# Out projection: upper half of the columns, first eight heads, as seven block products per pair of K tiles, summed in PSUM

## The chip, the core and the metric

One core of one Trainium2 chip runs the kernel. The metric is the device time of one execution in microseconds (us), as the median of several. TensorE (PE in the profile) multiplies, with its weight loads listed apart (PEld); VectorE (DVE) and ScalarE (ACT) do elementwise work; GpSimd (POOL) and SyncE (SP) here mostly issue transfers, which sixteen DMA engines carry out. PSUM, the memory that TensorE writes, has eight banks of 128x512 float32.

## What is computed

The reference is one decoder layer on 256 rows of 2048 columns: a mixing part and a feed-forward part, each with a norm before and behind it. The change is in the projection that closes the mixing part, the line with `w_out`.

```python
h = rmsnorm(x, pre_mix_gain[layer])
proj = jnp.einsum('bsd,de->bse', h, w_in[layer])
q_sb, k_sb, v_sb, q_dl, k_dl, v_dl = jnp.split(proj, splits, axis=-1)
o_sb = head_rmsnorm(stick_breaking_attention(...), sb_out_gain[layer])   # 8 heads of 128
o_dl = head_rmsnorm(dilated_attention(...), dil_out_gain[layer])         # 8 heads of 128
mixed = jnp.concatenate([o_sb, o_dl], axis=-1)                           # 256 x 2048
mix_out = jnp.einsum('bse,ed->bsd', mixed, w_out[layer])                 # 2048 x 2048
x = x + rmsnorm(mix_out, post_mix_gain[layer])
h = rmsnorm(x, pre_ffn_gain[layer])
f = conv_geglu_ffn(h, w_up[layer], conv_w[layer], conv_b[layer], w_down[layer])
x = x + rmsnorm(f, post_ffn_gain[layer])
```

## The kernel before

**Arithmetic.** Every large float32 product is taken apart. An operand is split into a high part (type fp32r) and the rest (low part), and one product becomes three matmuls: high by high, low by high, high by low. For a weight tile `raw` of 128x1024, ACT makes the high part (`wh`, function `high`, L139) and DVE subtracts it from the raw tile (`wl`, function `low`, L146).

**Staging.** Weights are streamed. The list `chunks` names them in order of use: V columns ("v"), query and key columns of each head ("qk"), out projection ("out", column block c of 512, K group kq of four K tiles), up projection ("up", 86 of them). A chunk is 128x2048, two raw tiles of 512 KB. The main loop takes one chunk at a time; `ahead` loads up to two chunks ahead, on SP's queue (L128), and splits one ahead. The raw tiles turn in a ring of five buffers, `wh` and `wl` in rings of four. A load is issued when its ring buffer has been split; a split waits until TensorE is done with the tile that held its `wh` and `wl` buffers.

**Out projection.** `mm_moving` multiplies one chunk with the mixed heads: `mix` holds their high and low parts with the K dimension on the partitions, 16 K tiles (one for each head) of 256 rows. For each K tile, each half t of the rows and each column block there are three matmuls of 128x512 (L207, L208, L211), 24 in a chunk, added up in one PSUM bank for each (c, t). The chunks run over columns 0 and 1, then 2 and 3. The last two chunks (c=3, kq=2 and 3) are held and done together, rows t=0 first, so that the norm of t=0 runs beside the matmuls of t=1. `rows.squares` (L573, ACT) and `rows.take` (L577, DVE) empty a bank; `update` (L1040) adds the residual `x1`, which was loaded at the start and stayed in SBUF; `turn` transposes it for the up projection. The attention of the last heads still runs in small pieces (`step`) beside the first out chunks; TensorE's order there was fixed when the program was built.

**Down projection and its sums.** The last stage (class `Down`) already uses seven block products in place of eight for pairs of K tiles. It needs sums of weight blocks, which are not in the input. They are made in DRAM, beside the earlier stages: for each pair a tile T13 (SP copies two blocks of 256 KB, `copy_blocks` L727; POOL adds a third block to each with two accumulating DMAs, `add_block` L731) and for some pairs a tile T24 (one copy, then two additions, one behind the other). I call one copy with its two additions a set. `presum`, called once for each chunk from the eighth on, does one step: T13 takes two steps, T24 three. Here there are 34 T13 and 23 T24, 137 steps in all.

Of the kernel before, what the change touches and what calls it, by code (L numbers as in the profile page):

```python
# [24 lines left out]
RAW_BUFS = 5  # L25
# [11 lines left out]
LATE_PAIRS = 2  # L37
HELD = 4
SINGLE_BEHIND = (0, 2, 4, 5, 7, 9, 11, 12, 14)

# [60 lines left out]
def layer_kernel(ctx: ExitStack, tc: tile.TileContext, a, out: bass.AP):  # L101
    nc = tc.nc
# [17 lines left out]
    HALF = 1024  # L120
    LOW_AT = 80

    def load(src, w, piece=HALF):
        raws = []
        for lo in range(0, w, piece):
            n = min(piece, w - lo)
            raw = wpool.tile([P, n], F32, tag="raw", name="raw", bufs=RAW_BUFS, padded_shape=[P, HALF])
            nc.sync.dma_start(raw, src[:, lo:lo + n])  # L128
            raws.append(raw)
        return raws  # L130

    def split(raws, kind):

        return [low(raw, high(raw, kind), kind) for raw in raws]
# [61 lines left out]

    def mm_moving(ps, parts, hi, lo, k0, first, last, ts=(0, 1)):

        k1 = k0
        for i, (wh, wl) in enumerate(parts):  # L200
            n = wh.shape[1] // 512
            for t in ts:
                tc_ = slice(t * P, (t + 1) * P)
                for j in range(n):
                    k = k1 + j
                    ws = wh[:, j * 512:(j + 1) * 512]
                    T.matmul(ps[t], hi[:, k, tc_], ws, start=(first and i == 0 and j == 0), stop=False)  # L207
                    T.matmul(ps[t], lo[:, k, tc_], ws, start=False, stop=False)  # L208
                for j in range(n):
                    k = k1 + j  # L210
                    T.matmul(ps[t], hi[:, k, tc_], wl[:, j * 512:(j + 1) * 512], start=False,  # L211
                             stop=(last and i == len(parts) - 1 and j == n - 1))
            k1 += n
# [17 lines left out]
    for gs in ((0, 1), (2,), (3,)):  # L231
# [6 lines left out]
    for c0, c1 in ((0, 1), (2, 3)):  # L238
        for c, kqs in ((c0, (0, 1, 2)), (c1, (0, 1, 2)), (c0, (3,)), (c1, (3,))) if c0 == 0 else ((2, (0, 1, 2, 3)), (3, (0, 1, 2, 3))):
            for kq in kqs:  # L240
                chunks.append(("out", c, kq, a["w_o"][c, kq], 2048))
    for j in range(FT):
# [5 lines left out]
    def ahead(i, splits=SPLITS):  # L248
        if i + LOADS >= len(chunks):
            down.load(2 * (i + 1 + LOADS - len(chunks)))  # L250
        if i + 1 == len(chunks):
            down.prepare(2)
        while len(raws) < min(len(chunks), i + 1 + LOADS):
            j = len(raws)
            if j in between:
                nc.sync.dma_start(*between[j])
            raws[j] = load(chunks[j][3], chunks[j][4])
        while len(parts_of) < min(len(chunks), i + 1 + splits):
            j = len(parts_of)
            parts_of[j] = split(raws[j], chunks[j][0])  # L260
        return parts_of[i]
# [13 lines left out]
    gpre = small.tile([P, KT], F32, name="gpre", bufs=1, padded_shape=[P, KT + 32])  # L275
    x1 = apool.tile([P, 2, D], F32, name="x1", bufs=1)
    x1_kept = nc.dram_tensor("x1_kept", (S, D), F32, kind="Internal").ap()
# [138 lines left out]

    vts = {}

    banks = []
# [23 lines left out]
    def stick_head(h, qk):  # L443
# [51 lines left out]
        if h == 0:  # L495
            V.tensor_scalar(gain[:, 0:NH], par[:, P_HEAD:P_HEAD + NH], -0.5, None, op0=ALU.mult)
        V.scalar_tensor_tensor(q, po, gain[:, h:h + 1], q, op0=ALU.mult, op1=ALU.mult)
        A.copy(mix[0][:, h, :], q)
        V.tensor_tensor(mix[1][:, h, :], q, mix[0][:, h, :].bitcast(F32), op=ALU.subtract)

# [175 lines left out]
    class Down:  # L676
# [15 lines left out]
        def __init__(self):  # L692
            self.units, self.tiles, self.presums, self.summed = [], [], [], []
            kept = [nc.dram_tensor(f"{n}_kept", (2, NPAIR, 2, P, HALF // 2), F32, kind="Internal").ap() for n in ("t13", "t24")]
            self.sums13, self.sums24, self.ticks = [], [], 0
            for cp in range(2):
# [35 lines left out]

        def presum(self):


            tick = self.ticks
            self.ticks += 1
            n, odd = divmod(tick, 2)
            if n < len(self.sums13):
                t13, blocks, b12 = self.sums13[n]  # L740
                if odd:
                    self.add_block(t13[0], b12)
                    self.add_block(t13[1], b12)
                else:
                    self.copy_blocks(t13, blocks)
                return
            tick -= 2 * len(self.sums13)
            for n, (t24, blocks, t13) in enumerate(self.sums24):
                at = tick - 3 * n
                if at == 0:  # L750
                    self.copy_blocks(t24, blocks)
                elif at == 1:
                    self.add_block(t24[0], t13[0])
                elif at == 2:
                    self.add_block(t24[1], t24[0])

# [199 lines left out]
    for i, (kind, p, s, _, w) in enumerate(chunks):  # L956
# [39 lines left out]
        elif kind == "qk":  # L996
# [7 lines left out]
            if s == 1:  # L1004
                active.append(stick_head(p, qk) if p < 8 else dilated_head(p, qk))
                next(active[-1])
        elif kind == "out":
            if s == 0:
# [4 lines left out]
            if p == 3 and s == 2:  # L1013
                held = parts
                continue
            if p < 3 or s < 2:
                mm_moving(mm["out", p], parts, mix[0], mix[1], 4 * s, s == 0, s == 3)
                if s == 3:
                    for t in range(2):
                        rows.squares(mm["out", p][t], t, p)  # L1020
                        rows.take(mm["out", p][t], t, p)
            else:
# [33 lines left out]
                def lows(b):  # L1056
                    for j in range(2):
# [3 lines left out]
                                                   op0=ALU.mult, op1=ALU.subtract))  # L1061

                for t in range(2):
                    mm_moving(mm["out", p], held + parts, mix[0], mix[1], 8, False, True, (t,))
                    if t == 1:
# [131 lines left out]
def _laid_out(inp):  # L1197
# [14 lines left out]
    for cp in range(2):  # L1212
        for kind, j in _down_plan(cp):
# [8 lines left out]
    w_first = np.concatenate([xT[n[0]] if len(n) == 1 else w_v[n[0], 0, :, n[1] * 512:(n[1] + 1) * 512]  # L1222
                              for names in OPENING for n in names], 1)
    arrays = {
        "x": x,
# [3 lines left out]
        "w_v": w_v,  # L1229
        "w_o": np.asarray(inp["w_out"])[0].reshape(4, 4, P, 4, 512).transpose(3, 0, 2, 1, 4).reshape(4, 4, P, 2048),  # L1230
        "w_up": np.asarray(inp["w_up"])[0].reshape(KT, P, 2, FT, P).transpose(3, 2, 1, 0, 4).reshape(FT, 2, P, 2048),
        "w_dn": w_dn,
# [20 lines left out]
```

## Time and profile before

| what | us |
|---|---|
| median of 3 runs | 1083.21 |
| the three runs | 1082.92, 1083.21, 1100.46 |
| the profiled execution, its whole time | 1082.44 |
| its span, first to last instruction | 1080.7 |
| out projection in that span, about | 293 to 386 |
| up projection, about | 389 to 861 |
| down projection and end, about | 861 to 1081 |

The granted TensorE clock was 0.998 of full speed over the span. A row of the profile's tables gives busy time, the mean duration of one instruction and the idle time before it; matmuls overlap, so the duration of one is more than the distance from one to the next. The three runs spread by 0.3 us without the one at 1100.46.

### The profile page before, as it was taken

What the parts mean: (1) busy time and instruction counts of PE and PEld (TensorE: products, weight loads), DVE (VectorE), ACT (ScalarE), POOL (GpSimd) and SP (SyncE); (2) the same over time, 40 slices, a digit from 0 to 9 for tenths busy, and PEclk for the clock granted to TensorE, in tenths of its full rate; (3) what the DMA queues carried; (4) which work ended last, traced back from release to release, by engine and by line L of the source; (5) the groups of instructions that cost most, each with busy time, mean ns of one, the idle gap of its engine ahead of it and who ended that gap; (6) DMA issues with size and microseconds to landing.
All of it is one profiled execution on the core that took longest, in us unless ns stands there. A gap on an engine that the chain in (4) does not pass through costs nothing.

```text
span 1080.7 us, 18925 instructions
## 1 busy us (share of the span) xinstructions
PE 1069.3 (99%) x7169; PEld 977.6 (90%) x7169; DVE 835.5 (77%) x1267; ACT 676.1 (63%) x991; POOL 96.7 (9%) x127
## 2 busy tenths in 40 slices
PE   9999999999999999999999999999999999999996
PEld 7888888988888889999999999999999988888885
DVE  7577766866865478887877878787787699998997
ACT  6657867756754385555555555555555587666775
POOL 0011111111111101111001001001000000000002
PEclk9999999999999999999999999999999999999999
DMA  9999889899889959998888888888888799779993
GB/s 352 358 289 282 242 239 282 245 271 253 249 259 282 268 207 301 296 285 265 255 262 263 257 248 266 262 255 260 263 243 272 210 340 380 270 265 355 395 361 120
DMA packets 96188, 297.88 MB, mean 276 GB/s; under 512 B 10400, under 2 KB 11168, under 8 KB 91680
## 3 DMA queue, kind: packets, MB, share of 16 engines
q1 hardware_dynamic: 90192, 266.24, 70.4%
q0 software_dynamic: 5472, 29.89, 16.7%
q8 instruction: 56, 0.92, 0.3%
q10 hardware_dynamic: 432, 0.53, 0.1%
q14 instruction: 36, 0.29, 0.1%
HBM read 292.43 MB, written 63.96 MB: 330 GB/s over the span
## 4 chain that ended last, share of the span: by engine, by line
PE 98%; DVE 1%; ACT 0%; issue 0%; DVEq 0%; ACTq 0%
PE mmu L171 42%; PE mmqk L161 11%; PE p L819 6%; PE p L818 6%; PE p L817 6%; PE mmqk L159 5%; PE mmv L207 3%; PE mmv L211 3%; PE mmv L208 3%; PE mmo L211 3%; PE mmo L208 3%; PE mmo L207 3%; PE mmu L182 1%; PE score L441 1%; PE idle L300 0%; PE head L441 0%
## 5 line engine op out<-in xcount | busy, mean ns | idle before, releaser
L146 DVE TENSOR_TENSOR wl<-raw,wh 128x1024 fp32r<-128x1024 f32 (+1 forms) x379 | 452.1, 1200 | 173.2 <-ACT wh L139 142.3
L139 ACT CAST wh<-raw 128x1024 fp32r<-128x1024 f32 (+1 forms) x379 | 389.4, 1033 | 176.4 <-PE mmu L171 60.8
L171 PE MATMUL mmu<-hT,wh 128*128 128x256 f32 x2688 | 311.9, 276 | 0.0
L171 PEld LDWEIGHTS mmu<-hT,wh 128*128 128x128 f32 x2688 | 308.1, 188 | 0.0
L171 PE MATMUL mmu<-hT,wl 128*128 128x256 f32 x1344 | 159.6, 276 | 0.0
L171 PEld LDWEIGHTS mmu<-hT,wl 128*128 128x128 f32 x1344 | 155.7, 188 | 0.0
L161 PE MATMUL mmqk<-hT,wh 128*128 128x512 f32 x512 | 121.8, 390 | 0.0
L161 PEld LDWEIGHTS mmqk<-hT,wh 128*128 128x128 f32 x512 | 94.9, 188 | 19.0
L637 ACT ACTIVATE cv<-pair,par 128x256 f32<-128x256 f32 x86 | 51.6, 600 | 81.2 <-DVE pair L635 80.9
L731 POOL DMA_DIRECT2D t_kept<-in_w x68 | 53.7, 918 | 409.5 <-DMA t_kept<-in_w_dn 409.5
L817 PE MATMUL p<-wh,yp 128*128 128x512 f32 x210 | 81.7, 389 | 0.0
L818 PE MATMUL p<-wh,yp 128*128 128x512 f32 x210 | 81.7, 389 | 0.0
L819 PE MATMUL p<-wl,yp 128*128 128x512 f32 x210 | 81.6, 390 | 0.0
L159 PE MATMUL mmqk<-hT,wl 128*128 128x256 f32 x512 | 67.0, 278 | 0.0
L731 POOL DMA_DIRECT2D t_kept<-t_kept x46 | 35.6, 775 | 338.5 <-DMA t_kept<-in_w_dn 206.1
L159 PEld LDWEIGHTS mmqk<-hT,wl 128*128 128x128 f32 x512 | 63.2, 188 | 1.3
L638 DVE SCALAR_TENSOR_TENSOR cv<-pair,par,cv 128x255 f32<-128x255 f32 x86 | 41.2, 479 | 15.2 <-ACT cv L637 15.2
L207 PE MATMUL mmo<-wh,mix 128*128 128x512 f32 x128 | 50.1, 391 | 0.0
L208 PE MATMUL mmo<-wh,mix 128*128 128x512 f32 x128 | 49.8, 389 | 0.0
L208 PE MATMUL mmv<-wh,hT 128*128 128x512 f32 x128 | 49.7, 390 | 0.0
L207 PE MATMUL mmv<-wh,hT 128*128 128x512 f32 x128 | 49.6, 390 | 0.1
L819 PEld LDWEIGHTS p<-wl,yp 128*128 128x128 f32 x210 | 39.4, 188 | 8.6 <-DVE wl L146 0.4
(242 smaller groups left out, 1290.7 us busy)
## 6 DMA issues: line engine op xcount, KB each, us to landing
raw<-in_w_up SPq DMA_DIRECT2D x172, 512.0 KB, 5.6
raw<-in_w_qk SPq DMA_DIRECT2D x64, 512.0 KB, 6.0
t_kept<-in_w_dn SPq DMA_DIRECT2D x57, 512.0 KB, 6.8
t_kept<-in_w POOLq DMA_DIRECT2D x68, 256.0 KB, 6.6
raw<-in_w_o SPq DMA_DIRECT2D x32, 512.0 KB, 5.6
raw<-in_w_dn SPq DMA_DIRECT2D x31, 512.0 KB, 6.8
raw<-t_kept SPq DMA_DIRECT2D x29, 512.0 KB, 6.6
raw<-in_w_v SPq DMA_DIRECT2D x28, 512.0 KB, 5.7
```

The lines of the kernel that those rows point to most:

```text
L139: pin(A.copy(wh, raw))
L146: pin(V.tensor_tensor(wl, raw, wh.bitcast(F32), op=ALU.subtract))
L159: T.matmul(ps[:, 0, :], w, h[:, k, 0, :], **edge)
L161: T.matmul(ps, w, h[:, k, :, :], **edge)
L171: pin(T.matmul(ps, w, h[:, k, part, :], start=(i == 0), stop=(i == 3 * KT - 1)))
L207: T.matmul(ps[t], hi[:, k, tc_], ws, start=(first and i == 0 and j == 0), stop=False)
L208: T.matmul(ps[t], lo[:, k, tc_], ws, start=False, stop=False)
L211: T.matmul(ps[t], hi[:, k, tc_], wl[:, j * 512:(j + 1) * 512], start=False, stop=(last and i == len(parts) - 1 and j == n - 1))
L731: tc.keep_in_program_order(G.dma_start(flat(to), flat(block), accum_op=ALU.add, max_dma_last_dim=8192))
L817: T.matmul(ps, yh, wh[:, cs], start=key not in self.begun, stop=False)
L818: T.matmul(ps, yl, wh[:, cs], start=False, stop=False)
L819: T.matmul(ps, yh, wl[:, cs], start=False, stop=self.left[key] == 0)
```

## The change

For the column blocks 2 and 3 and the K tiles 0 to 7 (the eight stick-breaking heads), the eight block products for a pair of K tiles (two K tiles, two halves of rows, two column blocks) become seven, by Strassen's scheme in Winograd's form. Four pairs take 4 x 7 x 3 = 84 matmuls in place of 4 x 8 x 3 = 96. All eight PSUM banks are taken: seven collect the seven products over the four pairs, and an eighth the rest of column block 3, rows t=1. DVE then adds banks to banks; the products of K tiles 8 to 15 go on in the same banks.

What comes with it:

- Sums of the heads' rows: behind each odd stick-breaking head four DVE sums of 128x128, one ACT copy and one DVE subtraction of 128x512 (`so`). They live where the residual `x1` stood, so `x1` is loaded again (2 MB) before the last out chunk.
- Sums of the weight blocks: four T13 and four T24 for the out projection are made in DRAM by the same steps as for the down projection, ahead of those. There are 157 steps now. The new chunks of kind "ts", "pa" and "pb" make no step; in the up projection every fourth chunk makes two. 29 copies came behind the first load of the up projection, now it is 41.
- New chunks: "pa" loads 768 KB of plain blocks for a pair, "pb" the 1 MB of sums; for the first two pairs the sums ("ts") are loaded and split early, beside the lower column blocks, into the room of `hT`.
- Four chunks of 1 MB (columns 2 and 3, kq 0 and 1) are gone; 3 MB of blocks and 4 MB of sums are loaded in their place.

```diff
+    def load_sums(kept):
...
+            nc.sync.dma_start(raw.rearrange("p (o c) -> p o c", o=2), src.rearrange("o p c -> p o c"))
...
+    def split_early(raws, m):
+        if not early:
+            early.extend(cpool.tile([P, SPLIT_EARLY, 2, HALF], F32R, tag=f"hT{i}", name=f"early{i}") for i in range(2))
...
+            A.copy(wh, raw)
+            V.tensor_tensor(wl, raw, wh.bitcast(F32), op=ALU.subtract)
...
+    out_cols(0, 0)
+    out_cols(0, 1)
+    out_sums("ts", 0)
+    out_cols(0, 2)
+    out_cols(1, 0)
+    out_sums("ts", 1)
+    for c, kq in ((1, 1), (1, 2), (0, 3), (1, 3)):
+        out_cols(c, kq)
+    for m in range(3):
+        out_raw(m)
+    out_cols(2, 2)
+    out_sums("pb", 2)
+    out_raw(3)
+    out_sums("pb", 3)
+    for c, kq in ((2, 3), (3, 2), (3, 3)):
+        out_cols(c, kq)
...
+        V.tensor_tensor(sums[:, 0, :], a11, a21, op=ALU.subtract)
+        V.tensor_tensor(sums[:, 1, :], a22, a21, op=ALU.subtract)
+        V.scalar_tensor_tensor(sums[:, 2, :], sums[:, 1, :], -1.0, a11, op0=ALU.mult, op1=ALU.subtract)
+        V.tensor_tensor(sums[:, 3, :], a12, sums[:, 2, :], op=ALU.add)
+        A.copy(so[0][:, m, 0, :, :], sums)
+        V.tensor_tensor(so[0][:, m, 1, :, :], sums, so[0][:, m, 0, :, :].bitcast(F32), op=ALU.subtract)
...
+            for m in range(OUT_PAIRS):
+                t13, at = kept_out[0][m], 1536 * m
+                yield lambda: self.copy_blocks(t13, a["w_op"][:, at:at + 1024])
+                yield lambda: [self.add_block(t13[i], a["w_op12"][m]) for i in range(2)]
+            for m in range(OUT_PAIRS):
...
+            def product(b, row, part, c):
...
+                T.matmul(seven[b], yh, wh, start=b not in begun, stop=False, **kw)
+                T.matmul(seven[b], yl, wh, start=False, stop=False, **kw)
+                T.matmul(seven[b], yh, wl, start=False, stop=True, **kw)
...
+                product(5, 4, t13, 0)
+                product(7, 1, t13, 512)
+                product(6, 5, t24, 0)
+                product(4, 3, t24, 512)
...
+                x1 = apool.tile([P, 2, D], F32, tag="x1", name="x1", bufs=1)
+                for t in range(2):
+                    nc.sync.dma_start(x1[:, t, :], a["x"][t * P:(t + 1) * P, :])
...
+                for n, (y, w) in enumerate(((mix[0], wh), (mix[1], wh), (mix[0], wl))):
+                    T.matmul(seven[8], y[:, 8, P:S], w, start=(n == 0), stop=(n == 2), **loose)
...
-        if i >= 7:
-            down.presum()
+        if i >= 7 and kind not in ("ts", "pa", "pb"):
+            down.presum(2 if kind == "up" and i % 4 == 0 else 1)
```

How rows moved, first on DVE where the query and key columns of the last head end and the out projection begins (`wl` is the split of a streamed tile, `qk` and `rot` the rotary step of head 15, `early` the early split of the sums). Before:

```order
L146 TENSOR_TENSOR wl<-raw,wh 128x1024
L1003 TENSOR_TENSOR qk<-mmqk,half 128x256
L146 TENSOR_TENSOR wl<-raw,wh 128x1024
L505 TENSOR_TENSOR qk<-qk,cosR 128x512
L506 TENSOR_TENSOR rot<-rot,sinR 128x512
L146 TENSOR_TENSOR wl<-raw,wh 128x1024
L507 TENSOR_TENSOR qk<-qk,rot 128x512
```

And after, at the same place on DVE:

```order
L168 TENSOR_TENSOR wl<-raw,wh 128x1024
L150 TENSOR_TENSOR early_3278<-raw,early_3278 128x1024
L1062 TENSOR_TENSOR qk<-mmqk,half 128x256
L168 TENSOR_TENSOR wl<-raw,wh 128x1024
L150 TENSOR_TENSOR early_3279<-raw,early_3279 128x1024
L560 TENSOR_TENSOR qk<-qk,cosR 128x512
L561 TENSOR_TENSOR rot<-rot,sinR 128x512
L168 TENSOR_TENSOR wl<-raw,wh 128x1024
L562 TENSOR_TENSOR qk<-qk,rot 128x512
```

Two subtractions of 128x1024 have come in ahead of the sum that ends head 15's rotary step. Next, TensorE behind the first out chunk, where it takes up that sum (`score<-qk`). Before:

```order
L527 MATMUL score_672<-ident,sm 128x128 x3
L512 MATMUL score_671<-qk 128x128
L441 MATMUL score_671<-qh 128x256
L207 MATMUL mmo<-wh,mix_82 128x512
L208 MATMUL mmo<-wh,mix_83 128x512
```

And after, at the same place on TensorE:

```order
L582 MATMUL score_672<-ident,sm 128x128 x3
L230 MATMUL mmo<-wh,mix_82 128x512
L231 MATMUL mmo<-wh,mix_83 128x512
L230 MATMUL mmo<-wh,mix_82 128x512
L567 MATMUL score_671<-qk 128x128
L231 MATMUL mmo<-wh,mix_83 128x512
L234 MATMUL mmo<-wl,mix_82 128x512
L481 MATMUL score_671<-qh 128x256
```

Three matmuls of the out projection now stand ahead of `score<-qk`. Last, SP's queue early in the up projection (`raw` the loads of 512 KB, `t_kept` the copies for the down projection's sums). Before:

```order
L128 DMA raw<-in_w_up 128x1024 x4
L727 DMA t_kept<-in_w_dn 128x2x512
L128 DMA raw<-in_w_up 128x1024 x4
L727 DMA t_kept<-in_w_dn 128x2x512
L128 DMA raw<-in_w_up 128x1024 x6
```

And after, at the same place on SP:

```order
L129 DMA raw<-in_w_up 128x1024 x4
L782 DMA t_kept<-in_w_dn 128x2x512
L129 DMA raw<-in_w_up 128x1024 x2
L782 DMA t_kept<-in_w_dn 128x2x512
L129 DMA raw<-in_w_up 128x1024 x4
```

Where a copy stood behind every four loads (every six, once T24 is made), some now stand behind two.

More of the change, by code (lines that the diff above doesn't have):

```diff
@@ L195, in mm_stationary_late, with mm_moving @@
             mm(1, k, 1, 0, start=False, stop=(k == KT - 1))
-    def mm_moving(ps, parts, hi, lo, k0, first, last, ts=(0, 1)):
+    def mm_moving(ps, parts, hi, lo, k0, first, last, ts=(0, 1), done=0, **kw):
         k1 = k0
@@ L417, in layer_kernel @@
     vts = {}
+    even, so = [None], []
     banks = []
@@ L1006, in layer_kernel @@
                 next(active[-1])
+        elif kind == "ts":
+            continue
+        elif kind in ("pa", "pb"):
+            if kind == "pa" and p == 0:
+                seven = {b: ps_at.tile([P, 512], F32, tag="at", name=f"o{b}") for b in (1, 5, 7, 6)}
+                seven |= {b: ps_mm.tile([P, 512], F32, tag="mm", name=f"o{b}") for b in (2, 4, 3, 8)}
+                mm["out", 2], mm["out", 3] = [seven[2], seven[4]], [seven[3], seven[8]]
+                begun = set()
+            def product(b, row, part, c):
+                if row in (1, 4, 5, 6):
+                    yh, yl = (so[0][:, p, i, max(row - 3, 0), :] for i in range(2))
+                else:
+                    k, t = divmod(row, 2)
+                    yh, yl = (x[:, 2 * p + k, t * P:(t + 1) * P] for x in mix)
+                wh, wl = (w[:, c:c + 512] for w in part)
+                kw = dict(skip_group_check=True)
+                T.matmul(seven[b], yh, wh, start=b not in begun, stop=False, **kw)
+                T.matmul(seven[b], yl, wh, start=False, stop=False, **kw)
+                T.matmul(seven[b], yh, wl, start=False, stop=True, **kw)
+                begun.add(b)
+            if kind == "pa":
+                rb, ra = parts
+                product(1, 0, rb, 0)
+                if p:
+                    product(3, 6, rb, 512)
+                product(2, 2, ra, 0)
+                if p == OUT_PAIRS - 1:
+                    u0, u1, u2 = mg[:, 0, 1536:2048], mg[:, 1, 1536:2048], mg[:, 1, 1024:1536]
+                    A.copy(u0, seven[1])
+                if p < SPLIT_EARLY:
+                    parts = [part for part in parts_of[next(j for j, c in enumerate(chunks) if c[:2] == ("ts", p))]]
+            if kind == "pb" or p < SPLIT_EARLY:
+                t13, t24 = parts
+                product(5, 4, t13, 0)
+                product(7, 1, t13, 512)
+                product(6, 5, t24, 0)
+                product(4, 3, t24, 512)
+                if p == 0:
+                    product(3, 6, rb, 512)
+                if p == OUT_PAIRS - 1:
+                    V.tensor_tensor(u1, seven[6], u0, op=ALU.add)
+                    V.tensor_tensor(u2, seven[5], u1, op=ALU.add)
+                    V.tensor_tensor(seven[3], seven[3], u2, op=ALU.subtract)
+            continue
         elif kind == "out":
@@ L1061, in lows @@
                                                    op0=ALU.mult, op1=ALU.subtract))
+                hT2 = Halves([cpool.tile([P, KT // 2, 2, S], F32R, tag=f"hT{i}", name=f"hT{i}") for i in range(2)])
+                hT = [Halves(hT2.tiles, i) for i in range(2)]
+                loose = dict(skip_group_check=True)
+                wh, wl = (w[:, 0:512] for w in held[0])
+                for n, (y, w) in enumerate(((mix[0], wh), (mix[1], wh), (mix[0], wl))):
+                    T.matmul(seven[8], y[:, 8, P:S], w, start=(n == 0), stop=(n == 2), **loose)
+                pin(V.tensor_tensor(seven[8], seven[8], u2, op=ALU.subtract))
+                rows.take(mm["out", 2][1], 1, 2)
                 for t in range(2):
-                    mm_moving(mm["out", p], held + parts, mix[0], mix[1], 8, False, True, (t,))
+                    mm_moving(mm["out", p], held + parts, mix[0], mix[1], 8, False, True, (t,), done=t, **loose)
                     if t == 1:
```

112 lines of the change are left out of this document (73 added, 39 removed).

## The prediction

> **What bounds the kernel now.** I read the page's busy times and chain first, then what TensorE waited for, then the starts of its matmuls in the out projection, then the other engines and the DMA engines stage by stage.
>
> ```profile
> span 1080.7 us, 18925 instructions
> PE 1069.3 (99%) x7169; PEld 977.6 (90%) x7169; DVE 835.5 (77%) x1267; ACT 676.1 (63%) x991; POOL 96.7 (9%) x127
> PE 98%; DVE 1%; ACT 0%; issue 0%; DVEq 0%; ACTq 0%
> PE idle L300 <- DVE warm L297: 1.2, 1, 1.2
> PE pth L1048 <- DVE x L1040: 1.2, 1, 1.2
> PE mmu L182 <- ACT hT L1054: 0.2, 1, 0.2
> 376.10 0.39 PE L207 MATMUL mmo<-wh,mix 128*128 128x512 f32 x1
> 384.26 0.39 PE L207 MATMUL mmo<-wh,mix 128*128 128x512 f32 x1
> 293.00:387.00 94.00, 94.00 (x439) 78.04 (x437) 54.84 (x85) 48.59 (x86) 11.03 (x14) 1.00 0.86 257
> ```
>
> TensorE is the bound from end to end: 98% of the chain, and all that it waited for are three waits of 2.6 us together, none inside the out projection. In the last row (window; PE, PEld, DVE, ACT, POOL busy; clock; DMA share; GB/s) it is busy for 94 of 94 us at full clock, DVE for 55. So a matmul taken out there shortens the run by one matmul, if nothing else comes late. Its price is the distance from start to start, not the 0.39 us that each lasts: between the two matmul rows lie six groups of six, 36 matmuls, in 384.26 - 376.10 = 8.16 us, which is 0.227 us each, and 24 in a chunk make 5.44 us.
>
> The page "TensorE: Matmul & The Clock Gate" of the Trainium skill (section "Back-to-back issue gap") gives about 131 ns for sustained matmuls of 512 columns; by it the twelve would be worth 1.6 us. This trace has 227 ns, and the measurement decides.
>
> **Part 1: twelve matmuls fewer.** 96 become 84; the split of the last block (three matmuls of K tile 8 done ahead, and left out later) moves matmuls without adding any. 12 x 0.227 = 2.7 us less.
>
> **Part 2: the early splits.** The two tiles of the first "ts" chunk are split while TensorE begins the out projection, ahead of head 15's rotary sum on DVE, for which TensorE has its place in a fixed order.
>
> ```profile
> L146 DVE TENSOR_TENSOR wl<-raw,wh 128x1024 fp32r<-128x1024 f32 x363 | 442.1, 1223 | 172.2 <-ACT wh L139 142.3 <-PE mmu L171 14.2 <-issue 7.7
> 295.66 1.23 DVE L146 TENSOR_TENSOR wl<-raw,wh 128x1024 fp32r<-128x1024 f32 x1 [0.52 <-ACT wh L139]
> 299.28 0.68 DVE L507 TENSOR_TENSOR qk<-qk,rot 128x512 f32<-128x512 f32 x1
> 300.77 0.39 PE L512 MATMUL score<-qk 128*128 128x128 f32 x2
> ```
>
> The sum ended at 299.96 and TensorE took it up at 300.77. Two subtractions of 1.22 us come in ahead of it, 0.52 us of which fall into an idle gap: it ends near 301.9. TensorE, with three out matmuls moved ahead, would come to it at 300.77 + 3 x 0.227 = 301.45. A wait of 0.5 us takes the place of none; between 0 (more gaps are used) and 1.0 (none is). The later "ts" chunk stands where the heads are nearly done; the low part of the next column tiles is behind it, needed 5.4 us later.
>
> **Part 3: the end of the projection.** With three matmuls moved ahead of t=0, t=1 has 21 instead of 24, so TensorE ends it 0.68 us sooner. What follows cannot all move with it.
>
> ```profile
> 384.96 0.62 ACT L573 ACTIVATE jks<-x 128x512 bf16<-128x512 f32 x1
> 385.88 0.60 ACT L573 ACTIVATE jks<-mmo 128x512 bf16<-128x512 f32 x1 [0.21 <-PE mmo L211]
> ```
>
> ACT squares a block of the new `x` first and waited only 0.21 us for TensorE's last matmul. The chain squares, norm, update, transposes therefore starts 0.2 us sooner, not 0.7: 0.5 us is given back (0 to 0.7).
>
> **Part 4: the stretch of sevens.** A "pb" chunk has 12 matmuls, 2.72 us, and needs two subtractions, 2 x 1.22 = 2.45 us; a late "pa" chunk has nine, 2.04 us, and needs one of 1.22 and one of 0.69.
>
> ```profile
> L146 DVE TENSOR_TENSOR wl<-raw,wh 128x512 fp32r<-128x512 f32 x16 | 11.0, 685 | 1.1 <-PE p L818 1.1
> q1 hardware_dynamic: 4953, 17.47, 92.7%
> DMA to landing us min/median/max: 3.5/5.7/10.3
> ```
>
> From the third "pa" to the second "pb" TensorE has 2.04 + 5.44 + 2.72 + 2.04 + 2.72 = 15.0 us of work. DVE has in it the splits of the next five chunks, 4 x 2.45 + 1.91, and one sum of banks of 0.69: 12.4 us. The loads of these chunks are 5.0 MB; in the first 50 us, where loads alone filled the engines, 17.47 MB took 92.7% of 50 us, 2.65 us for a MB, so 13.2 us. Both fit, with 2 to 3 us to spare, and each split has its buffers free 1 to 3 us before TensorE needs it. I take 0; a load that lands at 10.3 instead of 5.7 us eats this and costs up to 3. The sums of banks that DVE does beside the next chunk (0.69 each) end ahead of the matmuls that go on in those banks.
>
> **Part 5: work that lies beside.** The heads' sums add to DVE, four times, four operations of 0.29 and one of 0.69 us; the stretch where the first heads run:
>
> ```profile
> L663 DVE TENSOR_TENSOR pair<-pair 128x128 f32<-128x128 f32 x17 | 4.9, 291 | 0.6
> 50.00:160.00 110.00, 110.00 (x655) 97.71 (x655) 81.07 (x128) 76.12 (x130) 14.16 (x18) 1.00 0.89 268
> x<-in_x SPq DMA_DIRECT2D x2, 1024.0 KB, 6.9
> ```
>
> 7.4 us go into 29 us of DVE's idle time there, while TensorE waits for nothing: 0, at most 2 if one insertion makes a split late. The second load of `x1` goes out when the last block sums are used; TensorE then has 24 + 3 + 24 matmuls, 11.6 us, before the first update, and two loads of 1 MB with two up tiles ahead are 3.1 MB x 2.65 = 8.3 us: 0, at most 2. Were that cover gone, the update and the transposes behind it would wait.
>
> **Part 6: the block sums in DRAM.** Twenty steps are put ahead of the down projection's. They run before 160 us in place of others and are read after 293 us, so they delay nothing; but the down projection's sums slide into the up projection: 41 copies there instead of 29, 12 sets more.
>
> ```profile
> 414.00:474.00 60.00, 60.00 (x532) 60.00 (x531) 50.04 (x83) 36.45 (x49) 8.35 (x11) 1.00 0.99 310
> 474.00:861.00 387.00, 387.00 (x3415) 386.92 (x3414) 300.70 (x460) 215.47 (x268) 35.13 (x46) 1.00 0.86 255
> q1 hardware_dynamic: 5024, 15.51, 67.8%
> q0 software_dynamic: 560, 3.02, 30.6%
> raw<-in_w_up SPq DMA_DIRECT2D x22, 512.0 KB, 6.0
> t_kept<-in_w POOLq DMA_DIRECT2D x10, 256.0 KB, 6.2
> t_kept<-in_w_dn SPq DMA_DIRECT2D x5, 512.0 KB, 7.7
> t_kept<-t_kept POOLq DMA_DIRECT2D x1, 256.0 KB, 4.9
> q1 hardware_dynamic: 33431, 107.79, 66.5%
> q0 software_dynamic: 2784, 15.21, 19.9%
> raw<-in_w_up SPq DMA_DIRECT2D x166, 512.0 KB, 5.6
> t_kept<-in_w_dn SPq DMA_DIRECT2D x29, 512.0 KB, 6.9
> ```
>
> Here is the one resource that has little to give. While T13 tiles were made beside the up projection (414 to 474, rows three to eight), the DMA engines were taken for 99%; later, with T24 (three steps), for 86%; the last four rows are 387 to 861. Price of a load in the first stretch: 67.8% of 60 us over 15.51 MB is 2.62 us for a MB, 1.4 us for 512 KB, a copy the same; an addition: 30.6% of 60 us over 11 is 1.67. A set is 1.4 + 2 x 1.67 = 4.7 us. Four up chunks last 21.8 us on TensorE and now bring eight loads and 2.5 sets: 11.0 + 11.8 = 22.8 us, 1.0 too much, where two sets made 20.4. This lasts as long as T13 is made: 35 steps at five in four chunks, seven times four chunks, 7 us. Against it stands the ring: a load is asked for 2.5 chunks ahead, 13.6 us, less 2.3 for cast and subtraction and 6.0 to land, 5.3 us to spare. What is left is 1.7 us, and the `wl` ring covers some of it: I take 0.8. The lower end is 0; the upper comes from the prices of the whole up projection (66.5% of 474 us over 107.79 MB, 1.53 us a load; 19.9% over 58 additions, 1.63): 24.2 us in four chunks, 2.4 too much, 17 less 5.3, 12 us.
>
> **Sum.** -2.7 + 0.5 + 0.5 + 0 + 0 + 0.8 = -0.9 us. The profiled execution's 1082.44 would become 1081.5; the median stands 0.77 above it, so 1082.3 us.
>
> **Rivals.**
>
> *The DMA engines become the bound while T13 is made (slower than before).* Same place as part 6. It decides once the excess passes the ring's 5.3 us by more than the 1.7 us that the other parts gain. For it: 99% already, with loads landing in 6.0 against 5.6 us. Against: TensorE waited for nothing there. Between the prices, 2 to 12 us instead of 0.8: 1083.5 to 1093.5. The page "DMA: Bandwidth & Descriptors" of the Trainium skill (section "Queues, rings and completion order") says that a DMA engine takes turns between the queues with work, packet by packet; by that rule more additions hold up the loads even while the loads alone would fit, and the trace bears it out by that 0.4 us alone. It counts with this rival.
>
> *Waits in the stretch of sevens or at the x1 load.* Parts 4 and 5 at their upper ends, 2 to 5 us: 1083.5 to 1086.5. For it: spare times of 1 to 3 us. Against: DVE and DMA both have less work there than TensorE.
>
> *The whole 2.7 us arrives.* If gaps swallow parts 2, 3 and 6: 1080.5.
>
> **Numbers.** Forecast and full gain, -2.7 to +0.3 us: 0.62. DMA-bound: 0.24. Waits in the sevens: 0.10. Several upper ends at once (12 + 3 + 2 + 2 + 1.7 + 2.7 would just pass 21.7 us): 0.03. Anything that gains over 21.7 us has no term here: 0.01. I leave out the upper half of the DMA rival and the mishaps, 0.16 together, so 1079.8 (1080.5 less the runs' 0.7 us spread) to 1088. Two per cent, 21.7 us, is about what a measurement of this kernel can tell from no change: faster 0.01, within 0.96, slower 0.03.
>
> **What would show it.** Right: 12 fewer matmuls and no TensorE wait above 1 us but the known ones; DMA share 0.95 or more for some 150 us of the up projection; the out stage near 92 us. Wrong: TensorE or ACT waiting for `raw<-in_w_up` in the up projection (the first rival); waits for `wl`, `wh` or `x` between the first "pa" and the transposes (the second); a wait at `score<-qk` well over 1 us (part 2).

## The result, and the profile after

| | before | after |
|---|---|---|
| median of six runs, us | 1083.07 | 1088.37 |
| lowest of the runs, us | 1082.54 | 1086.66 |
| profiled execution, us | 1082.44 | 1087.02 |
| its span, us | 1080.7 | 1085.2 |

The changed kernel takes 1.0052 times as long (95% interval 1.004 to 1.0063): 5.6 us slower by this ratio, where I had forecast 0.9 us faster. Some executions of most kernels here, the one before too, are about 18 us longer and are left out of all comparisons and medians; where only such an execution was profiled (runs 1, 4, 6, 9, 14 and 17), the added time lies in the up projection, and the starts and waits up to there are still read.

The page of the profile after: the span, the busy times and the shares of the chain.

```profile
span 1085.2 us, 19025 instructions
PE 1069.1 (99%) x7157; PEld 977.0 (90%) x7157; DVE 852.7 (79%) x1303; ACT 683.8 (63%) x1004; POOL 108.9 (10%) x143
PE 92%; DVE 3%; DMA 2%; ACT 2%; issue 1%; DVEq 0%; ACTq 0%
```

The twelve matmuls are gone (7157 instead of 7169). TensorE's share of the chain fell from 98 to 92%, and DMA and ACT have come into it. What TensorE waited for:

```profile
PE pth L1164 <- DVE x L1156: 4.9, 1, 4.9
PE idle L339 <- DVE warm L336: 1.2, 1, 1.2
PE score L567 <- DVE qk L562: 0.7, 2, 0.4
PE score L481 <- ACT qh L474: 0.2, 1, 0.2
```

The wait at the transposes of `x` was 1.2 us before. To see how much each stage gives or takes, I lay the starts of a few of TensorE's instructions beside each other, first those of before (first matmul of the out projection, transposes of rows t=0, of t=1, first matmul of the down projection):

```profile
294.11 0.39 PE L207 MATMUL mmo<-wh,mix 128*128 128x512 f32 x1
385.62 1.47 PE L1048 MATMUL pth<-ident,x 128*128 128x128 f32 x12
388.26 0.83 PE L1048 MATMUL pth<-ident,x 128*128 128x128 f32 x4 [1.17 <-DVE x L1040]
860.54 0.40 PE L817 MATMUL p<-wh,yt 128*128 128x512 f32 x1
```

The same after, with the two waits at `score<-qk` (the rotary sum of heads 8 and 9):

```profile
203.68 0.49 PE L567 MATMUL score<-qk 128*128 128x128 f32 x2 [0.30 <-DVE qk L562]
216.73 0.49 PE L567 MATMUL score<-qk 128*128 128x128 f32 x2 [0.37 <-DVE qk L562]
295.36 0.39 PE L230 MATMUL mmo<-wh,mix 128*128 128x512 f32 x1
384.87 1.47 PE L1164 MATMUL pth<-ident,x 128*128 128x128 f32 x12
391.25 1.12 PE L1164 MATMUL pth<-ident,x 128*128 128x128 f32 x4 [4.90 <-DVE x L1156]
864.79 0.40 PE L876 MATMUL p<-wh,yt 128*128 128x512 f32 x1
```

| stage | before | after | change, us |
|---|---|---|---|
| start to first out matmul | 294.11 | 295.36 | +1.25 |
| out projection, to the transposes of t=0 | 91.51 | 89.51 | -2.00 |
| to the transposes of t=1 | 2.64 | 6.38 | +3.74 |
| up projection | 472.28 | 473.54 | +1.26 |
| rest | 220.16 | 220.41 | +0.25 |
| sum | 1080.7 | 1085.2 | +4.50 |

The first 1.25 us are lost at the two waits at `score<-qk`: counted instruction by instruction, TensorE is level with the kernel before until 203 us, 0.5 to 0.7 us behind it after the first of them and 1.2 us after the second.

The up projection's two windows, the first while T13 is made, which stood at 0.99 and 0.86 of DMA share before:

```profile
414.00:474.00 60.00, 60.00 (x529) 59.96 (x528) 49.87 (x80) 35.47 (x46) 11.83 (x16) 1.00 0.99 326
474.00:861.00 387.00, 387.00 (x3417) 387.00 (x3416) 303.02 (x466) 217.89 (x271) 50.70 (x66) 1.00 0.94 284
```

TensorE is busy throughout both. So the gain is there, and two places that I had priced at nothing, one ahead of the out projection and one at its end, take more than it. The chain of waits through the second place, in order of time (start, us, what):

```profile
372.20 14.88 DMA raw<-in_w_up
...
387.16 0.04 ACT wh L161
...
388.86 0.70 ACT jks L628 x2
...
390.70 0.50 DVE x L1156
391.20 0.05 issue
391.25 0.70 PE pth L1164 x2
```

ScalarE's timeline there (without its short reads and the small operations of the norm):

```profile
381.63 1.98 ACT L161 CAST wh<-raw 128x1024 fp32r<-128x1024 f32 x2
387.16 1.04 ACT L161 CAST wh<-raw 128x1024 fp32r<-128x1024 f32 x1 [3.54 <-DMA raw<-in_w_up]
388.11 0.62 ACT L628 ACTIVATE jks<-x 128x512 bf16<-128x512 f32 x1
388.86 0.60 ACT L628 ACTIVATE jks<-o 128x512 bf16<-128x512 f32 x1
```

And SP's queue, which issued the two loads of `x1` just ahead of that load of an up tile:

```profile
370.85 0.99 SPq L1122 DMA_DIRECT2D x<-in_x  x2
372.20 6.57 SPq L129 DMA_DIRECT2D raw<-in_w_up  x3
```

The up tile needed 14.88 us to land, behind 2 MB. In that stretch the DMA engines, which had been taken for two thirds of the time before, were taken for all of it (before and then after; second last: DMA share, last: GB/s):

```profile
371.00:387.00 16.00, 16.00 (x78) 13.27 (x76) 8.13 (x16) 7.66 (x14) 1.61 (x2) 1.00 0.66 195
```
```profile
371.00:387.00 16.00, 15.34 (x74) 12.64 (x73) 13.37 (x22) 6.36 (x12) 1.56 (x2) 1.00 1.02 365
```

TensorE does not want that tile yet. But its cast stands on ScalarE ahead of the square of the last block (`jks<-o`), and the norm, the updates and the transposes of t=1 come out of that square. `x1` itself was in time for t=0 (TensorE did not wait at 384.87), though its first half landed 11.2 us after its request, at 382.07, just ahead of VectorE's first update at 382.21. The third loss follows from the late transposes. The window 389 to 396, before and then after; third from the end is the granted clock:

```profile
389.00:396.00 7.00, 6.77 (x57) 6.47 (x57) 7.00 (x14) 6.79 (x18) 0.00 (x0) 1.00 0.80 282
```
```profile
389.00:396.00 7.00, 4.62 (x26) 4.11 (x27) 6.35 (x15) 5.16 (x15) 0.00 (x0) 0.76 0.57 235
```

When TensorE took up work again, it ran at a lower clock, 0.50 in the window from 392 to 394. That is the 1.26 us of the up projection, where it waits for nothing: counted from the transposes of t=1, its 30th instruction is already 1.25 us later than in the kernel before, and the lag stays at 1.27 us to the end of the stage.

### The profile page after: what moved, and what is told of

It is laid out like the page before. It is cut to its first block, busy times and chain, and to the rows that moved or that the text cites. A ratio compares the mean times of both kernels' runs of the same rounds, so it can differ in the third digit from the quotient of the medians.

```text
span 1085.2 us, 19025 instructions
## 1 busy us (share of the span) xinstructions
PE 1069.1 (99%) x7157; PEld 977.0 (90%) x7157; DVE 852.7 (79%) x1303; ACT 683.8 (63%) x1004; POOL 108.9 (10%) x143
## 4 chain that ended last, share of the span: by engine, by line
PE 92%; DVE 3%; DMA 2%; ACT 2%; issue 1%; DVEq 0%; ACTq 0%
PE mmu L193 42%; PE mmqk L183 9%; PE p L878 6%; PE p L877 6%; PE p L876 6%; PE mmqk L181 5%; PE mmv L230 3%; PE mmv L231 3%; PE mmv L234 3%; DMA raw<-in_w_up 1%; PE mmo L234 1%; PE mmo L230 1%; PE mmo L231 1%; PE mmu L204 1%; DMA raw<-in_w_o 1%; DVE wl L168 1%
## 5 line engine op out<-in xcount | busy, mean ns | idle before, releaser
L168 DVE TENSOR_TENSOR wl<-raw,wh 128x1024 fp32r<-128x1024 f32 x383 | 454.5, 1194 | 161.2 <-ACT wh L161 129.9
L161 ACT CAST wh<-raw 128x1024 fp32r<-128x1024 f32 x383 | 391.8, 1029 | 178.2 <-PE mmu L193 62.9
L877 PEld LDWEIGHTS p<-wh,yp 128*128 128x128 f32 x210 | 39.4, 188 | 8.3
L876 PEld LDWEIGHTS p<-wh,yp 128*128 128x128 f32 x210 | 39.4, 188 | 8.2
```

The lines of the kernel that those rows point to most:

```text
L161: pin(A.copy(wh, raw))
L168: pin(V.tensor_tensor(wl, raw, wh.bitcast(F32), op=ALU.subtract))
L876: T.matmul(ps, yh, wh[:, cs], start=key not in self.begun, stop=False)
L877: T.matmul(ps, yl, wh[:, cs], start=False, stop=False)
```

## The experiments

Theory A: the load of the up tile, held up by the reload of `x1`, holds up ScalarE's cast, and the cast the norm. Within it, the load may be late by its place in SP's queue (A1) or by bandwidth, whatever the queue (A2). Theory S: the sums of the heads' rows cost the 1.25 us ahead of the out projection. Rivals: the block sums in DRAM (B), the order that the build now gives (O).

**1. No reload** (`x1` set to zero on GpSimd)

```diff
-                    nc.sync.dma_start(x1[:, t, :], a["x"][t * P:(t + 1) * P, :])
+                    G.memset(x1[:, t, :], 0.0)
```

> The 2 MB reload of the residual x1 is left out (x1 is set to zero on GpSimd, so the residual of the first norm is missing). Nothing else moves on TensorE, VectorE or ScalarE. Theory A (the reload delays the up load behind it on SP's queue, ScalarE's cast of that tile waits, and norm, update and transposes wait behind the cast): the wait at the transposes of x falls from 4.9 to about 1.2 us, the clock stays at 1.00 behind it, and the whole is 3.7 + 1.3 = 5.0 us shorter than the changed kernel, about 1083.4. Rival B (the wait comes from the T13 sums in DRAM or from the new order in the projection): the wait stays near 4.9, the time within 1 us of 1088.

The kernel leaves out the residual. Median 1082.40 us, ratio to before 0.9999 (0.999 to 1.0008), wait at the transposes 1.5 us, up tile landed after 8.1 us. A holds for the place and the size; B falls.

**2. The cast moved** behind the squares and the norm

```diff
-                        hs.append(high(raws[i + 2][0], "up"))
                         square(0, 0)
...
+                hs.append(high(raws[i + 2][0], "up"))
                 hs.append(high(raws[i + 2][1], "up"))
```

> Only the cast of the second up chunk's first tile moves on ScalarE, behind the squares, the norm and the first transposes' casts; the reload stays. Theory A (the cast in front of the norm is what turns a late load into a TensorE wait): the wait at the transposes falls to 1 to 2.5 us, 1083 to 1085 us in all; the load itself still takes about 15 us to land. Rival A2 (x1 itself is late, or the wide load slows everything alike): the wait stays above 3.5 us, 1087 or more. Rival B as for the run without the reload: no change, 1088.

1083.69 us, ratio 1.0009 (0.9998 to 1.0019). The tile still took 14.5 us to land, but with the reload in place the wait is back at its old size:

```profile
PE pth L1164 <- DVE x L1156: 1.3, 1, 1.3
```

So it is the cast's place in ScalarE's order that turns the late load into a wait of TensorE.

**3. Sums of heads 6 and 7 left out, and 4. the same sums on GpSimd**

```diff
-        m = h // 2
+        if (m := h // 2) == 3: return
...
```
```diff
-        V.tensor_tensor(sums[:, 0, :], a11, a21, op=ALU.subtract)
...
+        (V if m < 3 else G).tensor_tensor(sums[:, 0, :], a11, a21, op=ALU.subtract)
...
```

> The sums of the fourth pair of heads (heads 6 and 7) are left out, and those of the third pair stand in for them, so the products of that pair are not the reference's. Theory S (these sums on VectorE and their copy on ScalarE push the casts and the rotary sums of heads 8 and 9 back, and TensorE waits at score<-qk): the first out matmul is back at 294.1 us from 295.4, 1.2 us shorter in all, about 1087.1. Rival (the first dilated heads would wait anyway, by the other order that the build now gives them): the first out matmul stays at 295 or later, no change.

> The same sums of heads 6 and 7, done on GpSimd in place of VectorE (their one copy stays on ScalarE), so that the result is the reference's again. Theory S: as without them, 1.0 to 1.3 us shorter than the changed kernel, first out matmul at 294.1 to 294.4. Rival (ScalarE's copy of the sums, or GpSimd's slower sums, hold the rest up): gain under 0.5 us, or a new wait at so<-sums or behind it.

Theory S missed both times. Left out (those of heads 4 and 5 stand in): 1088.75 us, first out matmul at 295.63, as in the changed kernel. On GpSimd: 1088.43 us, first out matmul at 296.23; ScalarE's copy of the sums now waited 1.0 us for GpSimd in its order. I had taken the wrong pair: the sums at 191 to 196 us are those of heads 4 and 5.

**5. Sums of the first pair alone**

```diff
+        if (m := h // 2): return
...
```

> Only the sums of the first pair of heads are made and stand in for the other three pairs, so the products of these are not the reference's. The run before it left out the pair of heads 6 and 7, whose sums come only at about 219 us; those at 191 to 196 us, ahead of the waits at score<-qk, belong to heads 4 and 5. Theory S2 (the sums of heads 4 and 5 push the rotary sums back): first out matmul at 294.1 to 294.5, 1.0 to 1.3 us shorter than the changed kernel, about 1087.2, no wait at score<-qk at 203 and 216. Rival O (the order that the build gave TensorE, or the early loads and splits, makes those waits): first out matmul stays at 295.3 or later, 1088.4.

The sums of the first pair stand in for the others. First out matmul at 294.30, no wait at `score<-qk`; 1086.79 us, one execution only. With these sums gone, 1.06 of the 1.25 us come back, and the 0.19 that is left is there within the first 10 us. O falls. The run leaves out three pairs; that it is the pair of heads 4 and 5 follows from the time of its sums and from run 3, which left out the pair behind it.

**6. All sums moved into the out projection, with the late cast**

```diff
...
+                if (kind, p, s) in SUMS_AT:
+                    pair_sums(SUMS_AT[kind, p, s])
...
```

> With the cast moved as before, the sums of all four pairs of heads are made in the out projection (beside its second to fifth chunk, from the mixed heads' high and low parts, which costs one addition of 128x512 more for each pair), so that the query and key stage is as it was. By theory S2 and the run with the late cast (1083.9): first out matmul at 294.1 to 294.5, and 1.2 us less, 1082.7, if VectorE's 10 us fit into its idle time of the first out chunks; 1083.9 to 1086 if they make a split late there. By rival O no change against 1083.9.

1088.25 us, 1.0047 (1.0031 to 1.0063): first out matmul at 294.69, but 18 us later a new wait of 3.9 us. ScalarE there:

```profile
311.54 1.04 ACT L150 CAST early<-raw 128x1024 fp32r<-128x1024 f32 x1 [4.02 <-DMA raw<-t_out]
312.49 0.40 ACT L578 ACTIVATE sm<-sm,m 128x128 f32<-128x128 f32 x1
```

It is the same pattern at the early block sums: a cast waits for its load, and the softmax of the last head (`sm`), which TensorE waits for, stands behind the cast.

**7. Early block sums later, with the late cast**

```diff
-    out_sums("ts", 0)
     out_cols(0, 2)
     out_cols(1, 0)
+    out_sums("ts", 0)
+    out_cols(1, 1)
     out_sums("ts", 1)
-    for c, kq in ((1, 1), (1, 2), (0, 3), (1, 3)):
+    for c, kq in ((1, 2), (0, 3), (1, 3)):
```

> With the cast moved as before, the two chunks of early block sums stand two and one chunks later among the lower columns, behind the last heads. Theory of part 2 (the early splits stand ahead of head 15's rotary sum): the waits of the last head's matmuls in the first out chunks (0.6 us in all) are gone, 1083.3. Rival: those waits come from the order of TensorE or the sums, 1083.9; or the splits are now late for the first sevens and TensorE waits there, 1084.5 or more.

1083.67 us, 1.0009 (0.9999 to 1.002), the same as with the late cast alone. The small waits of the last head move (0.3 us at another of its matmuls) rather than vanish.

**8. The reload on GpSimd's queue, twice, and 9. split over two queues**

```diff
-                    nc.sync.dma_start(x1[:, t, :], a["x"][t * P:(t + 1) * P, :])
+                    G.dma_start(x1[:, t, :], a["x"][t * P:(t + 1) * P, :])
```
```diff
-                    nc.sync.dma_start(x1[:, t, :], a["x"][t * P:(t + 1) * P, :])
+                    (nc.sync, G)[t].dma_start(x1[:, t, :], a["x"][t * P:(t + 1) * P, :])
```

> The reload of x1 goes out on GpSimd's queue instead of SP's; bytes and all else stay. Theory A1 (order: the up load waited in the queue behind 2 MB): the up tile that was 14.9 us in landing lands sooner, the wait at the transposes falls below 3 us, 1083.5 to 1086. Rival A2 (bandwidth: 2 MB more have to pass through the DMA engines in those 15 us, whichever queue they come from): the tile still takes 12 us or more, or x1 is now late in its place, the wait stays at 4 or above, 1087 to 1091.

> The reload of x1 on GpSimd's queue once more, for its median, since the first time gave one undisturbed run, 1082.45. Theory A1 (order in SP's queue): 1082.2 to 1083.2. Rival A2 (bandwidth): 1086 or more.

> As changed, but the first half of the reload on SP's queue and the second on GpSimd's. Theory A1 (what stands ahead in the same queue decides): the up tile behind 1 MB lands 2 to 4 us sooner than behind 2 MB, which is enough, a wait of 1.2 to 2 us at the transposes. On GpSimd's queue alone the second half was issued only when the first had landed, 9 us later, and the times spread over 5 us; here both go out at once, so the spread should fall: 1082 to 1083.5. Rival A2 (bandwidth): a wait of 3 us or more, 1086.

On GpSimd's queue: 1082.45 us in one execution the first time; the second time 1084.04 us, 1.001 (1.0001 to 1.0018), between 1081.4 and 1086.6, so neither what A1 nor what A2 had forecast. The wait was 1.3 us in both profiles. Split: 1087.56 us, 1.0051 (1.0036 to 1.0066). GpSimd's issues with the whole reload, then ScalarE's cast and VectorE's update of t=0 with the split one:

```profile
369.09 0.60 POOL L1122 DMA_DIRECT2D x<-in_x  x1 [27.94 <-PE o L1084]
380.38 0.55 POOL L1122 DMA_DIRECT2D x<-in_x  x1 [10.69 <-issue]
```
```profile
387.69 1.05 ACT L161 CAST wh<-raw 128x1024 fp32r<-128x1024 f32 x1 [3.69 <-DMA raw<-in_w_up]
385.87 2.74 DVE L1156 SCALAR_TENSOR_TENSOR x<-mg,rs,x 128x512 f32<-128x512 f32 x4 [3.29 <-DMA x<-in_x]
```

With both halves under way from two queues, the cast of the up tile began as late as with 2 MB in one queue (387.7 against 387.2). The split also made `x1` itself late: the half on SP's queue landed after 14.6 us, the update waited for it, and TensorE waited at the transposes of t=0 as well as of t=1 (1.25 and 3.13 us). On GpSimd's queue alone the second half went out 11 us after the first, when that had landed; the up tile then took 9.9 us, and TensorE had its short wait. So order in SP's queue (A1) falls as the whole cause: it does not fit the split. Bytes under way when the tile is asked for (A2) fit all three placements; this is argued from them, not tried by itself. Why the times on GpSimd's queue spread so was not settled.

**10. All sums on GpSimd, from the mixed heads, reload on its queue**

> The reload on GpSimd's queue, and all sums of heads made by GpSimd from the mixed heads' high and low parts, its own copy included, in a room that nothing else uses then, so that neither VectorE nor ScalarE has them in its order. By theory S2 (VectorE's and ScalarE's part of the sums pushes the rotary sums back): first out matmul at 294.1 to 294.5 and 1.1 us less than with the reload alone, 1081.3 to 1081.6 by the one undisturbed run. Rival (GpSimd's work slows VectorE, or the build finds another order that waits elsewhere): 1082.4 or more.

1087.40 us, 1.0041 (1.0027 to 1.0055), first out matmul at 298.94. The rival holds: GpSimd's work slows VectorE. An addition of GpSimd, a subtraction of VectorE beside it, and the same subtraction later, when GpSimd's sums were over:

```profile
120.44 1.29 POOL L547 TENSOR_TENSOR gbc<-mix,mix 128x512 f32<-128x512 f32 x1 [21.81 <-DVE mix L540]
120.60 1.55 DVE L502 TENSOR_TENSOR spl<-sp,sph 128x384 fp32r<-128x384 f32 x1 [0.25 <-ACT sph L500]
134.96 0.56 DVE L502 TENSOR_TENSOR spl<-sp,sph 128x384 fp32r<-128x384 f32 x1 [0.25 <-ACT sph L500]
```

Of the eight such subtractions, the two that fell beside GpSimd's sums took 1.54 and 1.55 us, the six others 0.55 to 0.56 us, as all eight did in the changed kernel.

**11 and 12. Denser block sums in DRAM**, for part 6 (reload on GpSimd's queue in both)

```diff
-            down.presum(2 if kind == "up" and i % 4 == 0 else 1)
+            down.presum(2 if kind == "up" and i % 2 == 0 else 1)
```
```diff
-            down.presum(2 if kind == "up" and i % 4 == 0 else 1)
+            down.presum(2 if kind == "up" else 1)
```

> The reload on GpSimd's queue, and three steps of block sums in every two up chunks in place of five in every four, so that they are denser and end sooner. Theory D (part 6: the prices of loads and additions add up, 11.0 us for eight loads and 4.7 for a set): 3 sets in four chunks are 25.1 us against 21.8, 3.3 too much for some six times four chunks, less 5.3 us of slack: about 14 us more than with the reload alone, 1096. Rival E (the shares count packets that wait for each other, so the prices are too high; only bytes count, 7.3 MB in 21.8 us, 337 GB/s, where 376 to 426 were seen around the reload): within 1 us of the reload alone, 1082 to 1083.5.

> The same with two steps in every up chunk. Theory D: 4 sets in four chunks are 29.8 us against 21.8; 8 too much for 4.4 times four chunks, and 1.7 too much later, less 5.3: 30 to 45 us more, 1112 to 1128. Rival E: 8.4 MB in 21.8 us are 385 GB/s, at the edge of the 376 to 426 seen: 0 to 8 us more, 1082 to 1091.

Three in two: 1082.54 us, 1.0001 (0.9991 to 1.001): E, not D. Two in one: 1096.19 us, 1.0127 (1.0114 to 1.014), 12 to 14 us more than the second try of run 8 and run 11, over E's 0 to 8 and far under D's 30 to 45. In its profile the up projection takes 484.1 us instead of 472.3 in that of run 8. The window 420 to 540 with three in two, then with two in one (second last: DMA share, last: GB/s):

```profile
420.00:540.00 120.00, 119.50 (x1051) 119.10 (x1050) 95.62 (x152) 68.08 (x88) 25.11 (x33) 1.00 1.03 338
```
```profile
420.00:540.00 120.00, 114.46 (x961) 112.27 (x960) 86.77 (x136) 60.32 (x78) 28.97 (x37) 1.00 1.04 336
```

The engines move 336 to 338 GB/s in both and no more; asked for 385, they make TensorE do 90 matmuls fewer in 120 us, and 90 x 0.114 (119.5 us over 1051) is 10 us. The changed kernel has 326 GB/s while it makes T13: nearly at this bound, but under it.

**13 to 15. Sums in pieces** (each piece a half step behind the last, in a room of their own), with the late cast

```diff
+        yield
         V.tensor_tensor(sums[:, 0, :], a11, a21, op=ALU.subtract)
         V.tensor_tensor(sums[:, 1, :], a22, a21, op=ALU.subtract)
+        yield
...
+        yield
         A.copy(so[0][:, m, 0, :, :], sums)
+        yield
...
```

> The late cast (1083.9 alone), and the sums of each pair of heads taken apart into four pieces, each a half step later than the one before, with a room of their own (the norm's gain tile, unused then). VectorE has the same operations in all. By theory S2 (a block of 1.8 us on VectorE with ScalarE's copy in it is what pushes the rotary sums of heads 8 and 9 back): first out matmul at 294.1 to 294.6, 1082.6 to 1083.1. Rival W (the work itself, 2 us for each pair, has no room there wherever it stands): first out matmul at 295.2 or later, 1083.9.

> The same with the first piece one whole step later. By S2: first out matmul at 294.1 to 294.6 too. By rival W: 295.2 or later. If the two runs differ by more than 0.5 us, it is neither the work nor the block but which single operation stands ahead of a rotary sum.

> Late cast, split reload and sums in pieces together. If each does what its theory says: first out matmul at 294.3, wait at the transposes 1.2, 1081.3 to 1082.0, which would be 1 us under the kernel before. If the pieces of sums do nothing: 1082.4 to 1083.

First out matmul at 294.11, 294.07 and 293.95: S2 against W, the work has room, its place had not. The first two took 1081.52 and 1083.94 us (two executions), and 1082.2 us (one). With the split reload: 1084.59 us, 1.0025 (1.001 to 1.0039), and a wait of 2.7 us at the transposes. The cast of the up tile was out of the way there; as in run 9 it was `x1` that came late, and VectorE's update of t=0 waited 1.96 us for it. Why the place of the sums matters shows on ScalarE (chosen rows), in the changed kernel and then with the pieces:

```profile
194.50 0.60 ACT L553 CAST so<-sums 128x512 fp32r<-128x512 f32 x1
195.78 1.03 ACT L161 CAST wh<-raw 128x1024 fp32r<-128x1024 f32 x1
197.28 2.00 ACT L161 CAST wh<-raw 128x1024 fp32r<-128x1024 f32 x2
199.31 0.62 ACT L558 COPY rot<-qk 64x512 f32<-64x512 f32 x1
```
```profile
194.67 1.04 ACT L161 CAST wh<-raw 128x1024 fp32r<-128x1024 f32 x1
195.61 0.61 ACT L557 CAST so<-gbc 128x512 fp32r<-128x512 f32 x1
197.58 0.62 ACT L563 COPY rot<-qk 64x512 f32<-64x512 f32 x1
198.85 2.18 ACT L161 CAST wh<-raw 128x1024 fp32r<-128x1024 f32 x2
```

In the block, the copy of the sums went ahead of a weight cast, and in the order of the new build two casts stand ahead of the rotary copies (`rot`), which start 1.7 us later; VectorE's rotary sum and TensorE's `score<-qk` follow. In pieces, the copies start at 197.58.

**16 and 17. Both remedies, for the interval**

> Late cast and sums in pieces once more, for the median: the first time gave two undisturbed runs, 1081.52 and 1083.94, the first matmul of the projection where it was before the change (294.11) and a wait of 1.3 us at the transposes. If both losses are gone and nothing else is left, the gain of the out projection, 1.5 to 2.0 us, should show: 1080.8 to 1082. If the clock falls behind the transposes in some runs, as it did in one profile with the late cast, 1082 to 1084 with a spread of 2 us or more.

> The same with the whole reload on GpSimd's queue. Split over two queues it helped nothing (the up tile landed at 387.7), so it is not the order within SP's queue but the bytes under way ahead of the tile; on GpSimd's queue alone the second half went out 10 us later. With the cast late, the up tile has time anyway; so by this reading the queue brings nothing more here, and may make x1 late: 1081 to 1085, not below the run beside it by more than 0.5 us.

Late cast and pieces: 1082.57 us, 1.0001 (0.9989 to 1.0012), from 1081.9 to 1084.2. With the reload on GpSimd's queue: 1082.14 us, 0.9994 (0.9982 to 1.0005). Neither is shown to be faster than the kernel before. In the profile of run 16 the out projection takes 89.74 us instead of 91.51, 1.8 us less, but the span is only 0.6 us shorter (1080.1 instead of 1080.7). Half of the rest is the price of the late cast itself, which TensorE waits for early in the up projection:

```profile
391.30 0.51 PE L204 MATMUL mmu<-hT,wh 128*128 128x256 f32 x2 [0.43 <-ACT wh L161]
```

The up projection is 0.63 us longer by it (the profiles of runs 7 and 13 have the same wait and lag; that of run 8's second try, with the cast in its old place, has neither). The remaining 0.5 us lies ahead of the out projection (0.17), at the transposes (0.15) and behind the up projection (0.22). Sums in pieces with the reload on GpSimd's queue and the cast in its old place were not tried together.

## Why the prediction was wrong

- **The step that failed** is part 5's second half: "TensorE then has 24 + 3 + 24 matmuls, 11.6 us, before the first update, and two loads of 1 MB with two up tiles ahead are 3.1 MB x 2.65 = 8.3 us: 0, at most 2". It counted only what lies ahead of the reload, and not what lies behind it: the next up tile was asked for 1.4 us later and took 14.88 us, and I had not looked who waits for that tile. That was ScalarE's cast, in front of the norm. Runs 1 and 2 show it. The sum was also too small for `x1` itself: its halves landed 11.2 and 14.5 us after their requests, not 8.3. A copy and two additions for the sums in DRAM, which the sum leaves out, were under way beside it. The first half came 0.14 us ahead of its update, where the sum leaves 3.3 us to spare, so "in time" was partly luck; in runs 9 and 15 it came late. From the forecast of -0.9 to the measured +4.5 in the span are 5.4 us: 3.24 here (3.74 instead of part 3's 0.5), 1.26 by the clock, 1.25 ahead of the projection, 0.2 in it and 0.25 behind the up projection, less the 0.8 of part 6. The clock had no term in the prediction.
- **Part 5, first half**, "7.4 us go into 29 us of DVE's idle time ... 0, at most 2": cost 1.25, inside its bound. A sum of idle time says nothing about order; run 13 shows that the work fits where it does not push the casts and the rotary copies.
- **Parts 1 to 4**: -2.7 + 0.5 = -2.2 was forecast for the out projection by parts 1 and 2, -2.0 measured. Part 3's 0.5 behind it was 0.15 where the cast does not stand in the way (2.79 us between the transposes in run 13, 2.64 before). The waits of the last head are there (0.2 us at `score` here), and they vary: from none to 2.3 us in the profiles that have this order of the early sums, 3.9 in run 6. Part 2 had named VectorE's subtractions; the long waits (runs 6 and 12) came from ScalarE's early cast waiting for its load. No profile shows the wait that part 2 describes, the one for the rotary sum. In the stretch of sevens TensorE waited for nothing, as part 4 said.
- **Part 6**, 0.8: the up projection shows no wait for it. The DMA share was 0.99 as forecast, but a set costs less than I took from shares of busy time, in which packets that share an engine may count twice (argued, not tried). By bytes, 326 GB/s against a bound of 337, it fits (runs 11 and 12). So the first rival did not come true, by a margin of 3%.
- **The ranges**: of the rivals, "waits in the sevens or at the x1 load", 1083.5 to 1086.5, was the one nearest to what happened, with 0.10. Its upper end left out the clock and the cast that waits for a tile nobody needs yet. 1088.37 lies 0.4 us above my range. The sum for the slower end is wrong: it adds the 2.7 us of the gain to the losses (20.7 us) where it should take them off, and so does not reach 21.7.

## What to carry to other kernels

A load that is added to a queue is to be priced for what comes behind it too: follow the next transfers to whoever waits for them, and look what stands behind that waiter in its engine's order. A cast that is done early, for later, belongs behind the work that the bottleneck engine is about to need, unless its load is sure to have landed. Small sums that fit into idle time on average still move others in a fixed order; in pieces they cost nothing here, in a block 1.2 us.

## What the hardware showed

- **A wait costs more than its length.** In all eight profiles in which TensorE waited 2.3 us or more inside the program (2.28, 2.66, 3.13, 3.93, 4.19, 4.88, 4.90 and 5.26 us), its granted clock was about 0.50 for some 3 to 6 us once it worked again; after waits up to 2.1 us it stayed at 1.00, but for the profile of run 2 (0.51 after a wait of 1.3). The spread of the changed kernel's six runs (3.2 us, against 0.7 before) fits this: the mean granted clock was 0.997 in the shortest and 0.994 in the three longest. It was not tried by itself.
- **GpSimd's sums slow VectorE's.** A subtraction of 128x384 took 1.54 to 1.55 us where one of GpSimd's sums ran beside it and 0.55 to 0.56 us in the same kernel where none did.
- **The DMA engines gave 336 to 338 GB/s** for loads, copies and additions mixed as here. Loads of 512 KB then took 11.4 us to land (run 12, 414 to 560 us) instead of 7.8 (changed kernel, 414 to 474). Around the reload, with loads for the most part, they gave 365 (changed kernel, 371 to 387).
